# The second block's last eight gate projections: from the recurrent scan to one stretch ahead of the neighbourhood attention

## The chip, the cores and the metric

The kernel runs on one core of a Trainium2 chip. It is written for five engines and their queues: TensorE (PE, with its weight loads PEld), VectorE (DVE), ScalarE (ACT), GpSimd (POOL) and SyncE (SP), which issues most transfers. The metric is the device time of one execution in microseconds (us). Before the change it is 2379.51 us, the median of three runs (2378.23 to 2380.06).

## The reference

Two blocks work on 1024 tokens of 1024 features in float32. The first block has an attention layer with a window of 128 and sinks, and a layer of moving means over 2 to 16 tokens. The second puts 16 learned tokens in front, projects all 1040 once with a matrix of 6144 columns, and runs two mixers on the result, a neighbourhood attention (NA) and a gated linear recurrence in both directions. Two gates of 1024 columns each, the last 2048 of the projection, weigh the two mixers' outputs:

```python
def second_block(...):
    h = jnp.concatenate([meta_tokens, x], axis=1)            # 16 + 1024 tokens
    a = rms_norm(h, norm_mix[l])
    (q_na, k_na, v_na, q_hg, z_f, z_b, i_hg, g_hg, gate_na, gate_hg) = split_cols(a @ w_in[l])
    y_na = neighbourhood_attention(q_na, k_na, v_na, na_rpb[l]) @ w_na_out[l]
    y_hg = hgrn2_branch(q_hg, z_f, z_b, i_hg, g_hg, lb_all[:, l], hg_norm[l]) @ w_hg_out[l]
    mix = jax.nn.sigmoid(gate_na) * y_na + jax.nn.sigmoid(gate_hg) * y_hg
    h = h + mix @ w_o[l]
    m = rms_norm(h, norm_mlp[l])
    h = h + jnp.square(jax.nn.relu(m @ w_up[l])) @ w_down[l]

def chunk_scan(q, k, v, log_f):     # S_t = diag(f_t) S_(t-1) + k_t v_t^T,  o_t = S_t^T q_t
```

`gate_hg` is the gate of the second branch. It depends only on `a`, which is complete before the neighbourhood attention starts, and it is used only after the scan, where the branches are mixed.

## The kernel before, in words

**A float32 product in three parts.** Weights and activations are each split in a rounded high part and the rest, and `mm3` (L104) adds three matmuls for each product: high by high (L108), high weight by low activation (L110), low weight by high activation (L111). A weight block of 1024 rows by 128 columns goes through `w_cols`: one 512 KB load on SP (`wraw`, three buffers), a cast on ACT (`whi`, L79) and a subtraction on POOL (`wlo`, L80).

**A projection.** `pieces_fm` (L187) gives 128 columns of `a @ w_in` for all tokens, feature-major, as a list of pieces. With `cut=1` a piece is one half of the tokens: 8 row blocks by 3 matmuls of 512 columns, 24 in all, into one bank of the accumulator. With `cut=2` a piece is 12 matmuls, two pieces to a bank. The pieces of the forward forget projection work on the 1040 tokens in three parts, two of 264 and one of 512 (`MTOK`).

**A gate.** `gate` (L565) is such a projection of 128 of the 2048 gate columns: 48 matmuls, two ACT activations (L569) into a staging tile, two stores into `d_gate` in DRAM (L570). Gates 0 to 7 are `gate_na`, 8 to 15 `gate_hg`. Their results are read back much later, by the phases that mix the branches.

**Where the sixteen gates stand.** Gates 0 and 1 end the phase before NA: they use that phase's accumulator pool of four banks and its staging tiles `z`, and PE has nothing else between them. Gates 2 to 7 are fill in NA. Gates 8 to 15 are 32 pieces of 12 matmuls, fill in the scan, with the scan's accumulator pool `psm` of two banks and four staging tiles `gate`.

**The scan.** Four heads follow each other. `Head` holds what a head does: three `projections` (forget gates of both directions, with products F and K on DVE in `forget`, L1026; and the query, `QS`), `out_gate` (`gs`), `meta_state`, `begin`, seven `level`s on both halves of the tokens, four `states`, two `output`s and two `finish`es (in `ends`). One `level` on one half (L1121) is an ACT copy `kc` (two buffers), four 128-column float32 matmuls `A` (L1129), and on DVE a predicated copy (L1131), the products `K` (L1133) and `Q` (L1134) and a small `t` (L1137). The next level of that half needs this level's `Q` and `K`. `finish` transposes on PE (L1192) and multiplies on DVE (`oh`, L1195).

`weave` (L1211) issues the steps of one head and spreads a list of fill pieces over them evenly, by count. The fill of heads 0 to 2 is ten or nine gate pieces, the head's own `out_gate` and the three projections of the next head, which are what the next head starts from; the first `finish`es of the head before are put among the steps. Head 3's fill has the last four gate pieces, its `out_gate`, the reloading of NA's output and the products `y_na`.

**What sets the order.** The program is written in the order of these calls. A scheduler then orders each engine's queue by what is ready and what comes free, so a piece or a load can move some way from where it is written; buffers (three `wraw`, two banks `psm`, two `kc`) limit how far.

Of the kernel before, what the change touches and what calls it, by code (L numbers as in the profile page):

```python
# [30 lines left out]
def fused_kernel(tc, a, out, stop=None, dbg=None):  # L31
# [176 lines left out]
    def run(calls):  # L208
        for c_ in calls:
            c_()  # L210
# [72 lines left out]
    with lay:  # L283
        with ExitStack() as ph:
# [4 lines left out]
            psm = ph.enter_context(tc.tile_pool(name="psm", bufs=6 - SB, space=PSUM))  # L289
# [173 lines left out]
            fill, ss, tm_ = {}, {}, {}  # L463
# [37 lines left out]
        psm = xp.enter_context(tc.tile_pool(name="psm", bufs=4, space=PSUM))  # L501
# [63 lines left out]
    def gate(ps_pool, pool, g, cut=1, bufs=2, name="gate", w=None):  # L565

        def ev(ps, sl):
            st = pool.tile([P, T if name == "z" else 512], F32, name=name, bufs=bufs)[:, :512]
            nc.scalar.activation(out=st, in_=ps, func=AF.Tanh if g < 8 else AF.Sigmoid, scale=0.5 if g < 8 else 1.0)  # L569
            nc.sync.dma_start(out=d_gate[g][:, sl.start - NM:sl.stop - NM], in_=st)  # L570
        return pieces_fm(ps_pool, x2, lambda: w or w_cols(w2, 4096 + g * P), ev, TOK, cut)
# [3 lines left out]
    with ExitStack() as ph:  # L575
# [164 lines left out]
        feature_major(1)  # L740
        gate0[1]()
        gate1[1]()
        with tc.issue_after(last[3].ins):
            wk0_ = w_cols(w2, 512)
    xp.close()
# [230 lines left out]
    with ExitStack() as ph:  # L976
# [273 lines left out]

        head = Head(0)
        run(head.projections())
        gates = [p_ for g in range(8, 16) for p_ in gate(psm, gp, g, 2, GB)]
        last = []
        for hh in range(3):
            nxt = Head(hh + 1)
            n = (10, 9, 9)[hh]
            fill = gates[:4] + head.out_gate() + nxt.projections() + gates[4:n]
            gates = gates[n:]
            st = head.scan()  # L1260
            weave(st[:5] + last + st[5:], fill)
            last = head.ends()
            head = nxt
        oo = XT()
        og, ona_, ohg = head.out_gate(), [(i, d_na[i]) for i in range(4)], [(4 + i, d_hg[i]) for i in range(3)]
        fill = gates[:2] + og[:2] + [lambda: load_o(0, ona_)] + gates[2:] + og[2:] + [lambda: load_o(1, ona_)]
        fill += [lambda d_=d_ + i, hf=hf: y_na(d_, hf) for d_ in range(0, 8, 2) for hf in range(2) for i in range(2)]
        fill.insert(18, lambda: load_o(0, ohg))
        fill.insert(20, lambda: load_o(1, ohg))
        st = head.scan()  # L1270
        weave(st[:3] + last + st[3:-1], fill[:-4])
        for c_ in (fill[-4], st[-1], fill[-3], *head.ends(), fill[-2], fill[-1]):
# [596 lines left out]
```

## Time and profile before

| | |
|---|---|
| median of three runs | 2379.51 us |
| the profiled execution, its own time | 2379.98 us |
| its span | 2378.2 us |
| PE busy | 2309.6 us (97%), 12054 matmuls |
| DVE busy | 1426.5 us (60%) |
| ACT busy | 971.5 us (41%) |
| POOL busy | 791.5 us (33%) |
| scan: first head's transpose to the end of the fourth head | 1195.1 to 1590.0 us |
| two gates ahead of NA: their last matmuls | about 785 to 790 us |

The page gives busy time by engine over the whole span, the same in 40 slices, and the costliest groups of instructions. A group names its line, engine, operation, output and inputs, then busy time and mean duration of one, then the idle time ahead of it. Busy time counts an instruction from its start to its end, and successive instructions of an engine overlap, so that of PE's short matmuls the distance between two starts, and not the duration of one, tells how fast the engine gets on.

### The profile page before, as it was taken

The page shows a single profiled execution, that of the slowest core. Times are in us where ns is not written, and L with a number is a line of the kernel's source. Part 1 is how long each engine was busy: PE and PEld are TensorE (multiplying, and loading weights), DVE is VectorE, ACT ScalarE, POOL GpSimd, SP SyncE. Part 2 cuts the span into 40 slices and gives each one's busy share as a digit, 9 for nine tenths or more (in the row PEclk, how much of TensorE's full clock was granted, in tenths as well). Part 3 has the DMA queues.
Part 4 walks back from the last instruction along what each step waited for, and adds up shares of the span by engine and source line. Part 5 has one row for each costly group of instructions (what it writes and reads, how often), then busy time and mean ns, then how long its engine had stood idle before and what let it go on. Part 6 is the DMA issues. An engine that isn't in the chain of part 4 may idle for free. (4 is left out here: it accounts for less than half of the span.)

```text
span 2378.2 us, 32052 instructions
## 1 busy us (share of the span) xinstructions
PE 2309.6 (97%) x12054; PEld 1921.4 (81%) x12054; DVE 1426.5 (60%) x2602; ACT 971.5 (41%) x1808; POOL 791.5 (33%) x528
## 2 busy tenths in 40 slices
PE   7999999999999999999999999999989999999997
PEld 6877777888887888878988888877768888878886
DVE  5566677654367255553265746759784444786775
ACT  5344452422226454543232232423555555533334
POOL 2112123112226343431212112126354444444455
PEclk9999999999999999999999999999999999999999
DMA  5111103111124222211111111467235444754331
GB/s 160 36 28 36 28 27 108 40 45 58 40 63 138 62 68 67 54 58 45 46 52 54 41 54 54 139 200 258 71 120 199 146 151 164 267 220 168 107 124 71
DMA packets 237147, 230.01 MB, mean 97 GB/s; under 512 B 59896, under 2 KB 179022, under 8 KB 233408
## 3 DMA queue, kind: packets, MB, share of 16 engines
q1 hardware_dynamic: 228176, 210.31, 27.5%
q10 hardware_dynamic: 8224, 16.00, 1.8%
q0 software_dynamic: 592, 1.65, 0.3%
q8 instruction: 95, 1.56, 0.3%
q14 instruction: 60, 0.49, 0.1%
HBM read 168.68 MB, written 59.24 MB: 96 GB/s over the span
## 5 line engine op out<-in xcount | busy, mean ns | idle before, releaser
L108 PE MATMUL mm<-xh,whi 128*128 128x512 f32 (+2 forms) x1744 | 670.9, 385 | 8.5 <-DVE st L1544 3.7
L110 PE MATMUL mm<-xl,whi 128*128 128x512 f32 (+2 forms) x1744 | 665.3, 382 | 0.0
L111 PE MATMUL mm<-xh,wlo 128*128 128x512 f32 (+2 forms) x1744 | 662.3, 380 | 2.3 <-POOL wlo L80 2.2
L80 POOL TENSOR_TENSOR wlo<-wraw,whi 128x1024 fp32r<-128x1024 f32 (+1 forms) x127 | 300.2, 2369 | 894.3 <-ACT whi L79 838.4
L108 PEld LDWEIGHTS mm<-xh,whi 128*128 128x128 f32 x1744 | 329.2, 189 | 70.2 <-issue 3.5
L111 PEld LDWEIGHTS mm<-xh,wlo 128*128 128x128 f32 x1744 | 329.3, 189 | 66.1 <-POOL wlo L80 3.4
L110 PEld LDWEIGHTS mm<-xl,whi 128*128 128x128 f32 x1744 | 329.4, 189 | 56.2
L79 ACT CAST whi<-wraw 128x1024 fp32r<-128x1024 f32 (+1 forms) x127 | 128.9, 1018 | 371.8 <-PE mm L110 174.3
L111 PE MATMUL mm<-whi,xl 128*128 128x512 f32 (+1 forms) x688 | 247.8, 360 | 0.0
L110 PE MATMUL mm<-wlo,xh 128*128 128x512 f32 (+1 forms) x528 | 184.6, 350 | 3.3 <-POOL wlo L119 2.6
L108 PE MATMUL mm<-whi,xh 128*128 128x512 f32 (+1 forms) x528 | 184.7, 350 | 2.1 <-DVE X L281 1.3
L111 PEld LDWEIGHTS mm<-whi,xl 128*128 128x128 f32 x688 | 130.7, 190 | 19.3
L108 PE MATMUL mm<-whi,xl 128*128 128x512 f32 x352 | 138.5, 394 | 4.7 <-ACT whi L118 2.4
L110 PE MATMUL mm<-wlo,xl 128*128 128x512 f32 x352 | 138.8, 394 | 3.9 <-POOL wlo L119 3.9
L1668 POOL TENSOR_TENSOR wlo<-raw,whi 128x1024 fp32r<-128x1024 f32 (+1 forms) x42 | 84.1, 2003 | 100.8 <-ACT whi L1667 100.8
L110 PEld LDWEIGHTS mm<-wlo,xh 128*128 128x128 f32 x528 | 99.8, 189 | 17.2 <-POOL wlo L119 3.9
L108 PEld LDWEIGHTS mm<-whi,xh 128*128 128x128 f32 x528 | 99.8, 189 | 15.4 <-DVE X L281 1.7
L119 POOL TENSOR_TENSOR wlo<-wraw,whi 128x1024 fp32r<-128x1024 f32 x30 | 80.6, 2692 | 80.4 <-ACT whi L118 78.0
L1595 DVE TENSOR_TENSOR st<-st 128x512 f32<-128x512 f32 x64 | 61.1, 975 | 57.8 <-ACT st L1581 56.8
L1791 DVE TENSOR_TENSOR X<-X,mm 128x512 f32<-128x512 f32 x112 | 73.1, 680 | 37.2 <-PE mm L111 37.2
L878 DVE CUSTOM_DVE_ANT_0 s<-S,bi 128x400 f32<-128x400 f32 x64 | 34.5, 571 | 94.6 <-PE S L870 94.6
L119 DVE TENSOR_TENSOR pl<-PT,ph 100x512 fp32r<-100x512 f32 (+2 forms) x128 | 83.6, 668 | 10.3 <-ACT ph L118 9.3
(370 smaller groups left out, 4400.1 us busy)
## 6 DMA issues: line engine op xcount, KB each, us to landing
wraw<-in_w_in_dram SPq DMA_DIRECT2D x48, 512.0 KB, 3.8
d_S<-st SPq DMA_DIRECT2D x64, 256.0 KB, 4.7
raw<-in_w_up_dram SPq DMA_DIRECT2D x30, 512.0 KB, 5.0
d_A<-st ACTq DMA_DIRECT2D x48, 256.0 KB, 2.0
fa<-d_S SPq DMA_DIRECT2D x10, 1024.0 KB, 4.9
wraw<-in_pool_w_in_dram SPq DMA_DIRECT2D x18, 512.0 KB, 3.9
fa<-d_A SPq DMA_DIRECT2D x9, 1024.0 KB, 4.8
wraw<-in_attn_w_in_dram SPq DMA_DIRECT2D x32, 256.0 KB, 3.2
```

Source lines behind the costliest of these rows:

```text
L79: nc.scalar.copy(out=hv[:, i:i + n], in_=view[:, i:i + n])
L80: nc.gpsimd.tensor_tensor(out=lv[:, i:i + n], in0=view[:, i:i + n], in1=f(hv[:, i:i + n]), op=ALU.subtract)
L108: nc.tensor.matmul(ps, lhsT=lh[0], rhs=rh[0], start=first and i == 0, stop=False, skip_group_check=chain)
L110: nc.tensor.matmul(ps, lhsT=lh[0], rhs=rh[1], start=False, stop=False, skip_group_check=chain)
L111: nc.tensor.matmul(ps, lhsT=lh[1], rhs=rh[0], start=False, stop=last and i == n - 1, skip_group_check=chain)
L119: return (lo_eng or nc.vector).tensor_tensor(out=lo, in0=src, in1=f(hi), op=ALU.subtract)
L878: nc.vector.tensor_tensor_reduce(out=s, in0=sps[j], in1=bs[j], scale=-0.125, scalar=-NEG, op0=ALU.add, op1=ALU.min, accum_out=mx)
L1595: return nc.vector.tensor_tensor(out=out_, in0=x_, in1=y_, op=op)
L1668: nc.gpsimd.tensor_tensor(out=lv, in0=view, in1=f(hv), op=ALU.subtract)
L1791: added[:] = [nc.vector.tensor_tensor(out=dst, in0=dst, in1=banks[t], op=ALU.add)]
```

## The change

The eight gates 8 to 15 are computed right behind gates 0 and 1, each as two pieces of 24 matmuls, in that phase's accumulator pool and with its staging tiles `z`. The fill lists of the scan lose their 32 gate pieces; what remains is `out_gate` and the next head's projections in heads 0 to 2, and `out_gate`, the reloads and `y_na` in head 3. The two places at which NA's later outputs are reloaded in head 3's list move up by four, the number of pieces that went. The arithmetic of a gate is the same.

```diff
--- before.py
+++ after.py
@@ -740,6 +740,8 @@
         feature_major(1)
         gate0[1]()
         gate1[1]()
+        for g in range(8, 16):
+            run(gate(psm, up, g, name="z"))
         with tc.issue_after(last[3].ins):
             wk0_ = w_cols(w2, 512)
     xp.close()
@@ -1250,23 +1252,20 @@
 
         head = Head(0)
         run(head.projections())
-        gates = [p_ for g in range(8, 16) for p_ in gate(psm, gp, g, 2, GB)]
         last = []
         for hh in range(3):
             nxt = Head(hh + 1)
-            n = (10, 9, 9)[hh]
-            fill = gates[:4] + head.out_gate() + nxt.projections() + gates[4:n]
-            gates = gates[n:]
+            fill = head.out_gate() + nxt.projections()
             st = head.scan()
             weave(st[:5] + last + st[5:], fill)
             last = head.ends()
             head = nxt
         oo = XT()
         og, ona_, ohg = head.out_gate(), [(i, d_na[i]) for i in range(4)], [(4 + i, d_hg[i]) for i in range(3)]
-        fill = gates[:2] + og[:2] + [lambda: load_o(0, ona_)] + gates[2:] + og[2:] + [lambda: load_o(1, ona_)]
+        fill = og[:2] + [lambda: load_o(0, ona_)] + og[2:] + [lambda: load_o(1, ona_)]
         fill += [lambda d_=d_ + i, hf=hf: y_na(d_, hf) for d_ in range(0, 8, 2) for hf in range(2) for i in range(2)]
-        fill.insert(18, lambda: load_o(0, ohg))
-        fill.insert(20, lambda: load_o(1, ohg))
+        fill.insert(14, lambda: load_o(0, ohg))
+        fill.insert(16, lambda: load_o(1, ohg))
         st = head.scan()
         weave(st[:3] + last + st[3:-1], fill[:-4])
         for c_ in (fill[-4], st[-1], fill[-3], *head.ends(), fill[-2], fill[-1]):
```

Three places show the order of the engines before and with the change. A name with a number is one allocated tile; `z` and `gate` are staging tiles of gates, `wraw` weight loads, `mm` an accumulator bank, `xh` and `xl` the two parts of the activations. In the scan and after it, lines of the changed kernel between L742 and L1252 are two higher (its L1131 is the level's matmul, L1133, L1135 and L1136 its copy, K and Q, L1194 and L1197 the transposes and `oh` of `finish`, L1037 the product of `gs`).

The first is SP's queue at the end of the phase ahead of NA, before the change, from the store of gate 0's second half (`z_7143`) on:

```order
L570 DMA d_gate_4831<-z_7143 128x512
L60 DMA wraw_7590<-in_w_in_2_dram 128x8x128
L570 DMA d_gate_4831<-z_7171 128x512
L60 DMA wraw_7801<-in_w_in_2_dram 128x8x128
L794 DMA be_7246<-d_rpb_4832 16x16x48 x8
L794 DMA be_7255<-d_rpb_4832 16x16x48 x8
L570 DMA d_gate_4831<-gate_7587 128x512
L60 DMA wraw_8096<-in_w_in_2_dram 128x8x128
```

With the change, from the same store on:

```order
L570 DMA d_gate_4831<-z_7143 128x512
L60 DMA wraw_7422<-in_w_in_2_dram 128x8x128
L570 DMA d_gate_4831<-z_7171 128x512
L60 DMA wraw_7484<-in_w_in_2_dram 128x8x128
L570 DMA d_gate_4831<-z_7205 128x512
L570 DMA d_gate_4831<-z_7233 128x512
L60 DMA wraw_7546<-in_w_in_2_dram 128x8x128
L570 DMA d_gate_4831<-z_7267 128x512
L570 DMA d_gate_4831<-z_7295 128x512
L60 DMA wraw_7608<-in_w_in_2_dram 128x8x128
L570 DMA d_gate_4831<-z_7329 128x512
```

The bias rows `be` of NA stood behind gate 1's two stores and one more weight load; now the stores of eight gates stand there, each pair of stores with one weight load behind it or between. Gate 8 works with `wraw_7174`, which is issued ahead of these rows; `wraw_7422`, `wraw_7484`, `wraw_7546` and `wraw_7608` are those of gates 12 to 15, and the rows `z_7205` and `z_7233` are gate 8's stores.

The second is PE's queue in head 1, from the first level on. Before the change (where lines are left out, rows of the piece ahead of them follow):

```order
L1129 MATMUL A_12437<-Q_12377,kc_12435 128x128 x4
L108 MATMUL mm_12453<-xh0_6817,whi_12449 128x512
...
L1129 MATMUL A_12468<-Q_12408,kc_12466 128x128 x4
L108 MATMUL mm_12453<-xh0_6817,whi_12449 128x512
...
L1192 MATMUL tp_12493<-ident_67,kt_12260 128x128 x4
...
L1192 MATMUL tp_12514<-ident_67,kt_12313 128x128 x4
L108 MATMUL mm_12501<-xh1_7065,whi_12449 128x512
...
L1129 MATMUL A_12538<-Q_12377,kc_12536 128x128 x4
L108 MATMUL mm_12554<-xh0_6817,whi_12550 128x264
...
L1129 MATMUL A_12569<-Q_12408,kc_12567 128x128 x4
```

With the change, from the last matmul ahead of the first level on:

```order
L111 MATMUL mm_12745<-xh1_7065,wlo_12690 128x512
L1131 MATMUL A_12760<-Q_12706,kc_12758 128x128 x4
L1131 MATMUL A_12772<-Q_12733,kc_12770 128x128 x4
L108 MATMUL mm_12745<-xh1_7065,whi_12689 128x512
...
L111 MATMUL mm_12745<-xh1_7065,wlo_12690 128x512
L1194 MATMUL tp_12796<-ident_67,kt_12617 128x128 x4
L1194 MATMUL tp_12823<-ident_67,kt_12666 128x128 x4
L1131 MATMUL A_12857<-Q_12706,kc_12855 128x128 x4
L1131 MATMUL A_12869<-Q_12733,kc_12867 128x128 x4
L1131 MATMUL A_12894<-Q_12706,kc_12892 128x128 x3
L108 MATMUL mm_12810<-xh0_6817,whi_12806 128x264
```

Before, each half of a level (`A_12437` and `A_12468`, then `A_12538` and `A_12569`) is followed by a piece of its own: twelve matmuls of `out_gate` (`mm_12453`, `mm_12501`) or a projection piece (`mm_12554`); four of the nine gate pieces stand ahead of them and the rest behind the projections. With the change both halves of the first level follow each other, then twelve matmuls of `out_gate` (`mm_12745`) and the two transposes of the finished head (`tp`), then both halves of the second level (`A_12857`, `A_12869`) and three of four matmuls of the third level's first half (`A_12894`), with no piece between.

The third is DVE's queue at that place with the change:

```order
L1133 COPY_PREDICATED A_12707<-lvl_11298,A_12760 128x512
L1136 TENSOR_TENSOR Q_12706<-Q_12706,F_12225 128x256x2
L1133 COPY_PREDICATED A_12734<-lvl_11298,A_12772 128x512
L1136 TENSOR_TENSOR Q_12733<-Q_12733,F_12345 128x256x2
L1135 TENSOR_TENSOR K_12226<-K_12226,t0_12768 128x128x2x2
L1135 TENSOR_TENSOR K_12346<-K_12346,t0_12780 128x128x2x2
L1197 SCALAR_TENSOR_TENSOR oh_12801<-tp_12796,gn_11291,gs_12098 128x512
L1197 SCALAR_TENSOR_TENSOR oh_12828<-tp_12823,gn_11291,gs_12098 128x512
L1133 COPY_PREDICATED A_12707<-lvl_11298,A_12857 128x512
L1136 TENSOR_TENSOR Q_12706<-Q_12706,t0_12768 128x128x2x2
L1037 TENSOR_TENSOR gs_12730<-gs_12730,mm_12693 128x512
```

The rows A, Q and K of numbers 12707, 12706 and 12226 are of one half, those of 12734, 12733 and 12346 of the other. The product Q of the second level (`t0_12768`), for which the third level's matmuls on that half wait, stands behind both halves' copies and products of the first level, both `oh` of the finished head and the second level's copy; the two products of `gs`, which free the accumulator banks of `out_gate`, stand behind it.

## Rows read from the trace of the kernel before

**Rows 1.** The page: span, busy time, share and count of each engine, and PE's busy tenths and granted clock in 40 slices of the span.

```profile
span 2378.2 us, 32052 instructions
PE 2309.6 (97%) x12054; PEld 1921.4 (81%) x12054; DVE 1426.5 (60%) x2602; ACT 971.5 (41%) x1808; POOL 791.5 (33%) x528
PE   7999999999999999999999999999989999999997
PEclk9999999999999999999999999999999999999999
```

**Rows 2.** Windows: the projections ahead of head 0, then the four heads, each from its `meta_state` transpose to the next one's. Columns: window and length in us; busy us and instructions of PE, PEld, DVE, ACT, POOL; granted clock, DMA share, GB/s.

```profile
1165.00:1195.13 30.13, 30.13 (x143) 25.02 (x142) 17.76 (x36) 7.06 (x15) 9.57 (x5) 1.00 0.24 70
1195.13:1294.21 99.08, 99.08 (x562) 85.39 (x561) 61.20 (x117) 31.95 (x66) 19.91 (x9) 1.00 0.16 48
1294.21:1391.51 97.30, 97.30 (x559) 83.94 (x558) 60.05 (x124) 31.05 (x65) 17.54 (x8) 1.00 0.17 52
1391.51:1492.19 100.68, 99.00 (x562) 84.83 (x561) 60.49 (x124) 29.84 (x64) 17.85 (x8) 1.00 0.15 48
1492.19:1590.00 97.81, 95.10 (x526) 80.63 (x524) 70.68 (x126) 33.65 (x66) 14.69 (x6) 1.00 0.51 167
```

**Rows 3.** Windows of the same columns: the level section of each head, from its first level matmul to its last level's end.

```profile
1208.74:1264.00 55.26, 55.26 (x318) 48.58 (x317) 42.16 (x71) 17.99 (x32) 12.78 (x6) 1.00 0.15 43
1307.81:1364.06 56.25, 56.25 (x326) 49.37 (x324) 42.22 (x73) 17.18 (x31) 10.38 (x5) 1.00 0.14 43
1405.13:1461.97 56.84, 56.62 (x320) 48.81 (x319) 40.35 (x67) 16.67 (x31) 9.48 (x4) 1.00 0.12 38
1506.30:1552.97 46.67, 46.67 (x258) 40.55 (x257) 43.89 (x62) 20.16 (x33) 9.30 (x4) 1.00 0.58 190
```

**Rows 4.** Waits of PE in the windows of head 2 (the first two rows) and head 3 (the other two): engine, output and line of what waited, engine, tile and line of what it waited for, us in total, times, the longest.

```profile
PE mm L108 <- DVE QS L1035: 1.5, 1, 1.5
PE mm L108 <- ACT K L1028: 0.2, 1, 0.2
...
PE tp L1149 <- ACT kt L1146: 2.2, 1, 2.2
PE tp L1192 <- DVE kt L1183: 0.2, 1, 0.2
```

**Rows 5.** Timeline of PE in head 1: two matmuls of a projection piece ten steps apart, then matmuls of `level`. Columns: start in us, duration in us, engine, line, operation; at the end the number of records of one instruction group.

```profile
1301.57 0.39 PE L110 MATMUL mm<-xl,whi 128*128 128x512 f32 x1
...
1303.88 0.39 PE L111 MATMUL mm<-xh,wlo 128*128 128x512 f32 x1
...
1307.81 1.49 PE L1129 MATMUL A<-Q,kc 128*128 128x128 f32 x8
...
1311.90 1.49 PE L1129 MATMUL A<-Q,kc 128*128 128x128 f32 x8
...
1329.58 1.05 PE L1129 MATMUL A<-Q,kc 128*128 128x128 f32 x8
...
1331.93 1.05 PE L1129 MATMUL A<-Q,kc 128*128 128x128 f32 x8
...
1345.72 1.05 PE L1129 MATMUL A<-Q,kc 128*128 128x128 f32 x8
...
1349.38 1.05 PE L1129 MATMUL A<-Q,kc 128*128 128x128 f32 x8
```

**Rows 6.** Timeline of PE in the stretch of gates 0 and 1 ahead of NA: two matmuls 24 steps apart.

```profile
785.01 0.39 PE L110 MATMUL mm<-xl,whi 128*128 128x512 f32 x1
...
790.45 0.39 PE L110 MATMUL mm<-xl,whi 128*128 128x512 f32 x1
```

**Rows 7.** Groups of ACT in the scan: the gates' activations.

```profile
L569 ACT ACTIVATE gate<-mm 128x512 f32<-128x512 f32 x16 | 9.5, 595 | 20.1 <-PE mm L111 20.1
```

**Rows 8.** The page's groups of a weight block's subtraction and cast (count; busy us, mean ns of one; idle time ahead and what ended it), and its line of the weight loads (count, KB each, us from issue to landing).

```profile
L80 POOL TENSOR_TENSOR wlo<-wraw,whi 128x1024 fp32r<-128x1024 f32 (+1 forms) x127 | 300.2, 2369 | 894.3 <-ACT whi L79 838.4
L79 ACT CAST whi<-wraw 128x1024 fp32r<-128x1024 f32 (+1 forms) x127 | 128.9, 1018 | 371.8 <-PE mm L110 174.3
...
wraw<-in_w_in_dram SPq DMA_DIRECT2D x48, 512.0 KB, 3.8
```

**Rows 9.** Timeline of POOL: the first product with the bias rows `be` in NA, and one weight subtraction in head 1's levels.

```profile
817.06 1.15 POOL L801 TENSOR_TENSOR bm<-be,rm 128x576 f32<-128x576 f32 x1
...
1340.37 2.39 POOL L80 TENSOR_TENSOR wlo<-wraw,whi 128x1024 fp32r<-128x1024 f32 x1 [14.44 <-ACT whi L79]
```

**Rows 10.** Timeline of DVE in head 1's levels: copy, Q and K of one half, and the product F of `forget` twice, in brackets the idle time ahead.

```profile
1334.04 0.72 DVE L1131 COPY_PREDICATED A<-lvl,A 128x512 f32<-128x512 uint8 x1
1334.66 0.67 DVE L1134 TENSOR_TENSOR Q<-Q,t 128x512 f32<-128x512 f32 x1
1335.26 0.67 DVE L1133 TENSOR_TENSOR K<-K,t 128x512 f32<-128x512 f32 x1
...
1340.82 2.22 DVE L1030 TENSOR_SCALAR F<-F,lb 128x512 f32<-128x512 f32 x1 [2.24 <-ACT F L1027]
...
1346.56 0.55 DVE L1030 TENSOR_SCALAR F<-F,lb 128x512 f32<-128x512 f32 x1 [1.29 <-ACT F L1027]
```

**Rows 11.** Groups of DVE in head 1's level section, forms apart: the first levels' product Q and the finished head's `oh`.

```profile
L1134 DVE TENSOR_TENSOR Q<-Q,F 128x512 f32<-128x512 f32 x2 | 2.3, 1129 | 0.0
L1195 DVE SCALAR_TENSOR_TENSOR oh<-tp,gn,gs 128x512 f32<-128x512 f32 x2 | 1.5, 750 | 3.4 <-PE tp L1192 3.4
```

## The prediction

> **What bounds the kernel now.** The page comes first: TensorE (PE) is busy 97% of a span of 2378.2 us, hardly a slice falls under 9 tenths, and the granted clock is near full in every slice [rows 1]. So nothing is to be won from the clock, and little from PE's idle time as a whole. Next come the windows of the four scan heads, each from one `meta_state` transpose to the next [rows 2]. Heads 0 and 1 (99.08 and 97.30 us) show PE busy for all of their time; head 2 has 99.00 of 100.68, head 3 95.10 of 97.81. VectorE (DVE) has 60 to 61 us in each of the first three and 70.7 in the last. Within a head the work is uneven: the seven levels on both halves take 46.7 to 56.8 us, and in them DVE is busy 40 to 44 us [rows 3]. This second fact decides the forecast, because the change removes PE work there and no DVE work. Last come PE's own waits [rows 4]: 1.5 + 0.2 us in head 2, 2.2 + 0.2 in head 3, none in heads 0 and 1.
>
> A busy PE in these records need not be a PE that gets on, so head 2 is compared with head 1. Both issue the same matmuls (but for two that belong to head 3), and head 2 takes 100.68 − 97.30 = 3.4 us longer. The waits show 1.7 of these; the whole 3.4 is stall. With head 3's 2.4 the scan holds **5.8 us** of stall now.
>
> **The change part by part.**
>
> *The matmuls.* A gate is 48 matmuls of 512 columns, eight gates 384, and all move. In the scan ten start-to-start steps take 1303.88 − 1301.57 = 2.31 us, 0.231 each [rows 5]: 384 × 0.231 = 88.7 us leave it. The dense stretch's nearest rows are the gates already computed at that place: 24 steps between 785.01 and 790.45, 0.2267 each [rows 6], or 87.05 us added. The sum of both is **−1.65 us**. Bounds: if the stretch ran at the scan's rate, 0; nothing in the rows is faster than 0.2267.
>
> *No switching to save.* A level step is four fp32 matmuls in eight records. From one to the next with a piece of twelve matmuls between takes 1349.38 − 1345.72 = 3.66 us [rows 5], 0.89 more than 12 × 0.231. With pieces of 264 columns between them it is 2.35 us [rows 5], and these pieces, too, leave about 0.9. I take the switch as part of the step; steps remain, and so does it.
>
> *Evacuation, weights, stores.* ScalarE's (ACT) sixteen sigmoids on gates in the scan took 0.595 us each [rows 7]; a half gate in the stretch is 24 × 0.2267 = 5.4 us of matmuls, so they are covered. A gate's weights need a load (3.8 us to landing), a cast (1.0) and GpSimd's (POOL) subtraction (2.4) [rows 8], 7.2 us in a row, against 10.9 us of PE for a gate. The order of SP shows each load standing several gates ahead of its use, so PE's work on the gates between hides it. Without that cover it would cost up to 7.2 × 8 = 58 us. The stores go with their gates. Behind them on SP stand the bias rows `be` of the neighbourhood attention, moved back by the stretch's length like all that follows; POOL first uses them at 817.06 [rows 9], 26 us after the last gate step of [rows 6], so projections still hide their loads. Before the scan, four `gate<-d_gate` loads now stand on SP ahead of weights; the 30.13 us of head 0's projections [rows 2] cover them. I put these edits at 0; the upper bound is one load that comes out late, 3.8 us.
>
> *What the scan loses as cover.* Heads 0, 1 and 2 give up 120, 108 and 108 matmuls, head 3 the remaining 48. By PE's order 72 of them stood in the levels of heads 0 and 1: PE then needs 55.26 − 16.6 = 38.6 us and 56.25 − 16.6 = 39.6. In head 3's levels it is 36: 46.67 − 8.3 = 38.4. Against these stand 42.2, 42.2 and 43.9 us of busy DVE [rows 3]. Busy time counts DVE's overlap twice: a predicated copy, a Q and a K of one half take 0.72 + 0.67 + 0.67 = 2.06 us by duration, but start 0.62 and 0.60 apart [rows 10], so about 1.82. Some fifty large operations in a head's levels give back 0.08 to 0.1 each, and the real occupancy is near 37 us. On top of it, DVE is held up by POOL: the F product takes 2.22 us while a weight subtraction runs, and 0.55 without [rows 9, 10]. So DVE and PE come out almost level, 37 to 41 against 39, and stalls depend on places.
>
> I go through the new order with these durations and those of [rows 11], 0.1 off each for the overlap. In head 1, with the first level at 0: its two halves now stand back to back (1.32 each: 4.09 between starts less a piece of 2.77 [rows 5]), then twelve matmuls and two transposes, the second level at 6.15 and 7.1, the third's first half due at 8.05. DVE has copy, Q, copy, Q, K, K until 5.9, two `oh` until 7.25, copy until 7.9; then Q, for which the third level waits, would end at 8.5. But the weight buffer came free with the twelve matmuls at 5.4, so cast and subtraction run until 9.0, and Q ends at 9.6. PE stands about 1.6 us; behind the waiting level are the 264-column projections, whose bank is free only after the `gs` product at 10.2, another 0.3. A second subtraction later in the levels costs about 0.6. That gives 2.5 for heads 1 and 2 each, 1.5 for head 0 (no `oh`; one delayed Q, one later), and for head 3 its old 2.4 plus 0.7 where the first two levels stand together. Sum **9.6 us** against 5.8 now: **+3.8 us**. Bounds: 2.4 (all but head 3's kt wait goes), and 16.7, derived below.
>
> **The sum** is −1.65 + 3.8 = +2.2 us. The profiled execution took 2379.98 us (span 2378.2, 1.8 around it), 0.47 over the median of the three runs; I add to the median and round up for the many small places I have not followed: **2382.0 us**.
>
> **Rivals.**
>
> *DVE becomes the bound of the levels (slower).* If PE can't run ahead at all, each head's levels last as long as DVE's busy time: +42.2 − 38.6 = 3.6, 42.2 − 39.6 = 2.6 twice, 43.9 − 38.4 = 5.5, with the 2.4 us of head 3 16.7. Less 5.8 and 1.65 that is +9.25, or 2389 us. For it: DVE's rows in head 3 stand nearly end to end already [rows 3], and two queues this evenly loaded seldom both stay full. Against it: half levels 2.35 us apart went through without a wait of PE [rows 4, 5], and the new mean distance is 39.6 / 14 = 2.8. It decides if a half level costs DVE, with the projections' evacuations and POOL's delays, over 2.8 us. The Trainium skill (Perfetto Trace Analysis, section Optimization Strategy) says that regimes with different busiest engines may gain from being interleaved, which speaks against this change; by that rule the time would be this rival's. Chance 0.31.
>
> *The gates were in the way (faster).* Head 2's extra 3.4 us came where a late gate piece and a QS product held one of two banks [rows 4]. If heads without gates all run like head 1 without its gates, the change gives −1.65 − 3.4 = −5.1, 2374.5 us; with head 3's wait gone too, 2372. Against it: the same engines have less cover. Chance 0.08.
>
> *The stretch isn't dense.* If weights arrive late, it costs up to 58 us, 2438 us; the order speaks against it. Chance 0.03.
>
> *Forecast*: within 0.2% (4.8 us, about what a measurement of this kernel tells from no change). Chance 0.58.
>
> **Numbers.** Faster by over 0.2%: 0.08; within: 0.58; slower: 0.31 + 0.03 = 0.34. The range reaches from 2376.0 (between forecast and the faster case) to 2391.0 (the DVE case, with 2 us more), and leaves out some 0.1 on the faster side and 0.08 above. The forecast's own range is 2377 to 2384.
>
> **What would show it.** Right: a stretch of 87 us before the attention with steps of 0.227 and no PE wait on `wlo`; heads 0 to 2 of 73 to 75.5 us each, head 3 of 86 to 89; DVE over 80% busy in the levels, PE's waits there put down to DVE's Q or to `gs`. Wrong: heads of 77 us and more, with DVE full from the first to the last level (the DVE rival); heads 1 and 2 alike at 72.5 and no waits (the faster one); waits on POOL or on a load in the stretch (not dense); or a change outside the stretch and the scan, which no step here foresees.

## The result, and the profile after

The changed kernel takes **2389.92 us** (median of five executions, 2387.18 to 2392.43) against 2379.74 of the kernel before beside it: a ratio of 1.0043 (95% interval 1.0028 to 1.0058), 10.2 us slower. That is inside the range forecast (2376 to 2391), but not the likeliest case (2382, no change that can be told): it is the side of the slower rival, which was given 2389 us and a chance of 0.31. The experiments show that the rival's number came about by other causes than the rival's. That the range holds the time is luck in part: it reached that far for a case that did not come about.

The page of the profiled execution (2389.92 us too), span and busy times [rows 1]:

```profile
span 2388.2 us, 32074 instructions
PE 2312.6 (97%) x12054; PEld 1925.0 (81%) x12054; DVE 1410.8 (59%) x2602; ACT 973.3 (41%) x1809; POOL 796.7 (33%) x528
```

Nothing on this page tells where 10 us went; 97% is what it was. So the stages come next. First the stretch ahead of the attention, from the last transposes before the gates to the first score matmul of the attention. Timeline of PE, kernel before:

```profile
780.46 0.60 PE L175 MATMUL tp<-ident,pp 128*128 128x128 f32 x4
...
825.55 0.46 PE L870 MATMUL S<-kh,qh 64*128 64x400 f32 x2
```

and the changed kernel:

```profile
780.21 0.60 PE L175 MATMUL tp<-ident,pp 128*128 128x128 f32 x4
...
913.57 0.45 PE L872 MATMUL S<-kh,qh 64*128 64x400 f32 x2
```

45.09 us have become 133.36: the eight gates cost **88.27 us**, 0.2299 for each of 384 steps. Where each half of gate 8 and the first half of gate 9 begin:

```profile
790.65 0.40 PE L108 MATMUL mm<-xh,whi 128*128 128x512 f32 x1
...
796.23 0.40 PE L108 MATMUL mm<-xh,whi 128*128 128x512 f32 x1
...
801.68 0.40 PE L108 MATMUL mm<-xh,whi 128*128 128x512 f32 x1
```

The 24 steps of the first half take 5.58 us, 0.233 each, those of the second 5.45, 0.227 each, and so it goes on in all eight gates. Then the scan: windows of the four heads [rows 2] and of the level sections of heads 0, 1 and 3 [rows 3]. The last window ends at the same place of PE's queue as in [rows 2], now at 1599.01:

```profile
1283.14:1357.90 74.76, 72.31 (x443) 63.15 (x442) 56.28 (x110) 26.60 (x52) 14.22 (x7) 1.00 0.10 29
1357.90:1432.23 74.33, 72.82 (x451) 63.97 (x449) 58.29 (x122) 26.01 (x58) 12.61 (x7) 1.00 0.12 36
1432.23:1506.64 74.41, 72.90 (x452) 63.96 (x450) 58.25 (x126) 24.12 (x56) 8.78 (x5) 1.00 0.08 29
1506.64:1599.01 92.37, 86.84 (x483) 73.24 (x480) 70.35 (x133) 33.36 (x71) 17.04 (x6) 0.98 0.49 157
...
1293.99:1331.55 37.56, 36.55 (x234) 33.13 (x233) 32.79 (x57) 13.59 (x25) 6.43 (x3) 1.00 0.10 29
1368.74:1407.71 38.97, 37.46 (x242) 33.99 (x241) 33.92 (x62) 13.89 (x26) 5.59 (x3) 1.00 0.13 41
1521.11:1565.25 44.14, 39.14 (x213) 33.44 (x212) 39.78 (x56) 18.30 (x28) 13.87 (x5) 0.96 0.59 187
```

Heads 0 to 2 lost 24.32, 22.97 and 26.27 us, head 3 5.44: **79.0 us**, where 384 steps of 0.231 are 88.7. So 88.3 came and 79.0 went, +9.3 of the 9.9 us between the two profiled executions; the remaining 0.7 lies in the first block and behind the scan, which differ from execution to execution (below). By heads the stall grew by 120 × 0.231 − 24.32 = 3.4 us in head 0, 2.0 in head 1, −1.3 in head 2 (its old 3.4 went) and 11.1 − 5.4 = 5.7 in head 3. PE's waits in the scan [rows 4]:

```profile
PE A L1131 <- ACT kc L1128: 3.9, 4, 1.3
PE mm L111 <- POOL wlo L80: 3.6, 1, 3.6
PE A L1131 <- DVE Q L1136: 1.5, 4, 0.8
PE tp L1146 <- DVE Sf L1156: 1.4, 1, 1.4
```

These waits don't make up the whole stall: they are 2.4 us of head 0's 3.4 and 1.5 in heads 1 and 2 each, where 2.0 were lost; the rest is not put down to any wait. The longest single wait is in head 3. Timeline of that place (POOL, DVE, then PE; some rows between are left out):

```profile
1525.63 4.91 POOL L80 TENSOR_TENSOR wlo<-wraw,whi 128x1024 fp32r<-128x1024 f32 x1 [37.42 <-ACT whi L79]
...
1525.87 2.46 DVE L119 TENSOR_TENSOR xl<-wraw,xh 128x512 fp32r<-128x512 f32 x4
1528.25 0.72 DVE L1133 COPY_PREDICATED A<-lvl,A 128x512 f32<-128x512 uint8 x1
1528.87 2.22 DVE L1135 TENSOR_TENSOR K<-K,t 128x512 f32<-128x512 f32 x1
...
1530.59 0.73 PE L111 MATMUL mm<-xh,wlo 128*128 128x512 f32 x1 [3.59 <-POOL wlo L80]
1531.12 0.63 PE L108 MATMUL mm<-xh,whi 128*128 128x512 f32 x1
...
1534.11 0.40 PE L110 MATMUL mm<-xl,whi 128*128 128x512 f32 x1
```

The first weights of `y_na` are subtracted while DVE makes four low parts of the reloaded attention output. The subtraction takes 4.91 us instead of 2.4 [rows 8], longer by about the 2.46 of the low parts, and in its turn stretches K from 0.67 [rows 10] to 2.22: K ends at 1531.09, 0.55 us behind the subtraction. PE stands for 3.59 us. And it doesn't end there: the next matmuls start 0.43 apart, not 0.23. Windows of these microseconds, with the granted clock in the third column from the end:

```profile
1528.00:1530.00 2.00, 0.00 (x0) 0.00 (x0) 2.00 (x3) 0.00 (x0) 2.00 (x1) 1.00 0.85 256
...
1531.00:1532.00 1.00, 1.00 (x4) 0.71 (x4) 0.69 (x2) 0.83 (x2) 0.00 (x0) 0.50 0.38 109
...
1534.00:1535.00 1.00, 1.00 (x8) 0.81 (x7) 0.22 (x1) 0.31 (x1) 1.00 (x1) 0.95 0.36 137
```

After the wait PE is granted 0.50 of its clock (1.2 of 2.4 GHz), and the full clock again early in the window from 1534 on (0.95). The eight steps from 1530.59 to 1534.11 took 3.52 us for 8 × 0.231 = 1.85: 1.7 more. This one late weight block cost 5.3 us.

In heads 1 and 2 the place is the one that the prediction walked through, the third level's first half. Timeline of head 1 there:

```profile
1374.12 1.05 ACT L79 CAST whi<-wraw 128x1024 fp32r<-128x1024 f32 x1 [1.84 <-PE mm L110]
1376.18 0.62 ACT L1128 COPY kc<-K 128x512 f32<-128x512 f32 x1 [1.02 <-PE A L1131]
...
1377.67 0.62 ACT L1128 COPY kc<-K 128x512 f32<-128x512 f32 x1
...
1375.29 2.37 POOL L80 TENSOR_TENSOR wlo<-wraw,whi 128x1024 fp32r<-128x1024 f32 x1 [16.33 <-PE tp L1194]
...
1376.82 1.39 DVE L1136 TENSOR_TENSOR Q<-Q,t 128x512 f32<-128x512 f32 x1
...
1378.36 0.91 PE L1131 MATMUL A<-Q,kc 128*128 128x128 f32 x6 [1.25 <-ACT kc L1128]
```

Cast, then subtraction, then a Q of 1.39 us (0.67 without, [rows 10]) that ends at 1378.21. The profile puts PE's wait down to the `kc` that ends at 1378.29. But `kc` has two buffers, and this half's copy is the one of 1376.18, the first behind the two of the second level, over at 1376.80; the one of 1377.67 is the other half's. So it is Q, held up by the subtraction, that PE waits for, as the prediction has it.

### The profile page after: what moved, and what is told of

The parts are those of the page before. It is cut to its first block, busy times and chain, and to the rows that moved or that the text cites. A ratio compares the mean times of both kernels' runs of the same rounds, so it can differ in the third digit from the quotient of the medians.

```text
span 2388.2 us, 32074 instructions
## 1 busy us (share of the span) xinstructions
PE 2312.6 (97%) x12054; PEld 1925.0 (81%) x12054; DVE 1410.8 (59%) x2602; ACT 973.3 (41%) x1809; POOL 796.7 (33%) x528
## 3 DMA queue, kind: packets, MB, share of 16 engines
q0 software_dynamic: 592, 1.65, 0.3%
## 5 line engine op out<-in xcount | busy, mean ns | idle before, releaser
L119 POOL TENSOR_TENSOR wlo<-wraw,whi 128x1024 fp32r<-128x1024 f32 x30 | 83.3, 2779 | 79.8 <-ACT whi L118 74.3
L119 DVE TENSOR_TENSOR pl<-PT,ph 100x512 fp32r<-100x512 f32 (+2 forms) x128 | 83.6, 667 | 10.2 <-ACT ph L118 9.2
```

The lines of the kernel that those rows point to most:

```text
L119: return (lo_eng or nc.vector).tensor_tensor(out=lo, in0=src, in1=f(hi), op=ALU.subtract)
```

## The experiments

The theory, called "places" in the expectations: PE-bound work was moved, so no time is won or lost by moving it; the loss is stall at a few places, where the pieces left no longer stand between two dependent steps. The rival, "DVE bound": without gates the levels last as long as VectorE's work in them, whatever the order.

All times in us; "before" is the kernel before beside each. "Middle" is the difference of the traces from the last transpose ahead of the gates to the last output matmul of the scan.

| kernel | median | before | ratio, 95% interval | middle |
|---|---|---|---|---|
| changed kernel | 2389.92 | 2379.74 | 1.0043 (1.0028 to 1.0058) | +9.3 |
| e1 fill in levels | 2383.08 | 2379.32 | 1.0017 (1.0008 to 1.0026) | +1.9 |
| e2 weights first | 2383.44 | 2379.32 | 1.0022 (1.0013 to 1.0031) | +4.3 |
| e3 gate 15 back | 2383.78 | 2379.32 | 1.0023 (1.0012 to 1.0033) | +2.9 |
| e4 gate 15 only | 2386.00 | 2379.32 | 1.0029 (1.0020 to 1.0038) | +7.7 |
| e5 both fixes | 2378.53 | 2378.77 | 0.9996 (0.9987 to 1.0005) | −1.8 |
| e6 both, head 3 by weight | 2377.36 | 2378.77 | 0.9996 (0.9987 to 1.0005) | −0.5 |
| e7 before, 10 8 10 | 2376.48 | 2378.77 | 0.9993 (0.9984 to 1.0002) | −3.4 |
| e8 gates twice | 2471.70 | 2378.77 | 1.0386 (1.0372 to 1.0401) | +88.5 |
| e9 split on VectorE | 2381.01 | 2378.76 | 1.0005 (0.9996 to 1.0015) | +2.1 |
| e10 e5 and e9 | 2378.47 | 2378.76 | 0.9997 (0.9987 to 1.0006) | −5.1 |
| e11 e10 again | 2377.00 | 2378.66 | 0.9992 (0.9983 to 1.0001) | −4.0 |
| e12 e7, split on VectorE | 2379.19 | 2378.66 | 1.0005 (0.9995 to 1.0014) | −2.5 |

The middle is the sharper measure: heads 0 to 2 of e10 and e11, one kernel traced twice, agree within 0.03 us, and those of the kernel before and of e8 are 99.08, 97.30 and 100.7 in both. Head 3 does not repeat so well: in e10 and e11 it took 75.72 and 76.66, so that a difference of 1 us in the middle tells nothing. The last transpose ahead of the gates stands anywhere from 777.9 to 783.1 in these traces, and what follows the scan's last transposes lasts 789.4 to 794.8.

**Spread the fill (e1).** In `weave`, for heads 0 to 2:

```diff
...
-                while done * len(steps) < (i + 1) * len(fill):
+                while done * sum(cost) < sum(cost[:i + 1]) * len(fill):
...
-            weave(st[:5] + last + st[5:], fill)
+            weave(st[:5] + last + st[5:], fill,
+                  [0, 1, 1] + [2] * 2 + [0] * len(last) + [2] * 12 + [1] * 4 + [1] * 2)
```

> The changed kernel with the fill of heads 0 to 2 spread by weight instead of by count: two shares for each half level, one for each begin, state and output, none for meta_state and finish. Same work, same eight gates ahead of the attention. Theory 'places': the scan loses its time at the few places where matmuls of two level halves stand together (waits for kc and Q of 0.92 + 0.42 in head 0, 1.43 + 0.42 in head 1, 1.42 + 0.42 in head 2, 5.0 us in all); with a piece behind each half they go, and heads 0 to 2 are 1.3, 1.8 and 1.8 us shorter: 2385 us. Some of it may come back at the states and outputs, which lose fill: up to 1.5 us each head. Rival 'DVE bound': the levels last as long as VectorE's work in them, whatever stands between; heads stay at 74.3 to 74.8 us, waits move to other levels: 2390 us.

Measured 2383.08. The heads of this kernel, and head 1's level section:

```profile
1360.35:1405.56 45.21, 45.21 (x279) 40.60 (x278) 38.38 (x71) 16.24 (x30) 6.17 (x3) 1.00 0.11 36
...
1283.38:1355.07 71.69, 71.44 (x443) 62.97 (x441) 53.81 (x98) 25.92 (x52) 13.75 (x7) 1.00 0.10 30
1355.07:1427.64 72.57, 72.34 (x451) 63.95 (x449) 57.77 (x124) 25.61 (x58) 12.53 (x7) 1.00 0.12 37
1427.64:1499.77 72.13, 72.13 (x451) 63.94 (x449) 57.39 (x129) 23.87 (x56) 8.95 (x5) 1.00 0.09 30
```

3.1, 1.8 and 2.3 us less; the waits in the levels are gone, and head 0's for `Sf` (1.4) is down to 0.25. VectorE is 85% busy in head 1's levels and holds nobody up. Nothing but the order of the pieces was changed, so without that order these stalls don't arise; e9 shows what else it takes.

**Head 3's weights (e2).** The first weights of `y_na` ahead of the reloads:

```diff
-        fill = og[:2] + [lambda: load_o(0, ona_)] + og[2:] + [lambda: load_o(1, ona_)]
+        def first_weights():
+            wn[0], wn[1] = pair_cols(w_na, 0)
+        fill = og[:2] + [first_weights, lambda: load_o(0, ona_)] + og[2:] + [lambda: load_o(1, ona_)]
```

(and the later two insertions one place on).

> The changed kernel with the first weights of y_na loaded and split ahead of the first reload of the attention's output, instead of behind both reloads; nothing else. Theory 'late weights in head 3': PE's wait of 3.6 us for wlo goes, since the subtraction (4.9 us beside four low parts on VectorE) no longer stands behind the reloads; head 3 is 3.0 to 3.9 us shorter: 2386.3 us. Rival 'head 3 is bound by VectorE': the wait moves to another tile (xl of the reloads, Q or kc) and less than 1 us is won: 2389 us or more.

Measured 2383.44. PE's waits in head 3, and its window to the last output matmul (82.2 us in the changed kernel):

```profile
PE A L1131 <- DVE Q L1136: 1.2, 1, 1.2
PE A L1131 <- ACT kc L1128: 0.7, 1, 0.7
```

```profile
1509.18:1586.50 77.32, 75.34 (x438) 64.64 (x436) 63.86 (x114) 29.05 (x59) 12.31 (x5) 1.00 0.55 167
```

4.9 us less, more than the 3.0 to 3.9 expected: with the wait the half clock went too (1.00 in the window). One new wait for Q of 1.2 us came.

**Which gate costs what (e3, e4).** e3 leaves gate 15 in head 3; against the changed kernel:

```diff
-        for g in range(8, 16):
+        for g in range(8, 15):
...
-        fill = og[:2] + [lambda: load_o(0, ona_)] + og[2:] + [lambda: load_o(1, ona_)]
+        gates = gate(psm, gp, 15, 2, GB)
+        fill = gates[:2] + og[:2] + [lambda: load_o(0, ona_)] + gates[2:] + og[2:] + [lambda: load_o(1, ona_)]
```

(and the later two insertions where they were before). e4 does the reverse; against the kernel before:

```diff
+        run(gate(psm, up, 15, name="z"))
...
-        gates = [p_ for g in range(8, 16) for p_ in gate(psm, gp, g, 2, GB)]
+        gates = [p_ for g in range(8, 15) for p_ in gate(psm, gp, g, 2, GB)]
...
-        fill = gates[:2] + og[:2] + [lambda: load_o(0, ona_)] + gates[2:] + og[2:] + [lambda: load_o(1, ona_)]
+        fill = og[:2] + [lambda: load_o(0, ona_)] + og[2:] + [lambda: load_o(1, ona_)]
```

(and the later two insertions as in the change).

> Gates 8 to 14 ahead of the attention as in the change, gate 15 back among the fill of head 3 as before. Theory 'places': head 3 has its old order and its old stall (2.3 us) in place of 5.9, the other heads stay: 2386.3 us, and no wait of PE for wlo in head 3. Rival 'every gate costs alike': the 10.2 us of the whole change are spread over eight gates, 1.3 us for this one: 2388.6 us.

> The complement: gate 15 alone ahead of the attention, gates 8 to 14 in heads 0 to 2 of the scan as before. Theory 'places': head 3 alone loses its cover, with the 3.6 us wait for wlo: 2379.7 + 3.6 = 2383.3 us. Rival 'every gate costs alike': 2381.0 us. The gains of this kernel and of the one with gate 15 back should add up to the whole change, 10.2 us.

2383.78 and 2386.00: gate 15 alone costs 6.7 us, the seven others 4.5; together 11.1, the whole 10.2. It is far from alike. Head 3 with gate 15 back, to the last output matmul; no wait for `wlo` is left in it, and its wait for `kt` is 1.4 (2.2 in the kernel before):

```profile
1493.74:1581.05 87.31, 85.90 (x487) 73.70 (x484) 65.77 (x114) 31.07 (x62) 14.63 (x6) 1.00 0.53 167
```

and without gate 15, the others in the scan:

```profile
1500.85:1585.65 84.80, 78.75 (x438) 67.21 (x437) 61.87 (x107) 29.33 (x53) 16.87 (x6) 0.96 0.55 174
```

To the same matmul head 3 of the kernel before takes 87.6; 84.80 is 2.8 us less for 11.1 us of matmuls taken out. Its waits are 3.0 for `wlo` and 2.8 put down to `kc`, its clock 0.96. I had expected 3.6 for e4 from the wait alone; the `kc` wait and the half clock were not in it.

**Both (e5), and head 3 too (e6).** e5 joins the two edits; e6 adds

```diff
-        weave(st[:3] + last + st[3:-1], fill[:-4])
+        weave(st[:3] + last + st[3:-1], fill[:-4],
+              [1, 1, 1] + [0] * 2 + [1] * 14 + [1] * 4 + [1])
```

> The changed kernel with both edits of the first experiments: fill of heads 0 to 2 by weight (one piece behind each half level), and the first weights of y_na ahead of the reloads in head 3. Theory 'places': the two losses are apart in time and add up. Heads as in the two traces, 71.7 + 72.6 + 72.1 + 77.3 = 293.7 us where the changed kernel has 305.7: 12 us less, 2378 us, level with or just under the kernel before. Rival 'DVE bound': what one fix wins the other loses, since VectorE's queue is the limit in sum: 2383 us as with each alone.

> As the kernel with both fixes, and head 3's fill by weight as well: one share for meta_state, each begin, half level, state and output, none for the two finishes. What is left of head 3's waits (Q 1.36, kc 0.82) stands where two halves follow each other; one such place goes. Theory 'places': 1 us under the kernel with both fixes, 2377 us. Rival: head 3 is at its bound by VectorE, no difference.

2378.53: the fixes add up, as expected. Heads 71.71, 72.56, 72.59 and 77.80 us. e6's 2377.36 cannot be told from it, and its trace does not show the 1 us that I expected: head 3 is 79.07, 1.3 longer, with a wait for Q of 1.5 and one for `kt` of 1.9.

**The kernel before had a stall of its own (e7).**

```diff
-            n = (10, 9, 9)[hh]
+            n = (10, 8, 10)[hh]
```

> The kernel before with 10, 8 and 10 gate pieces in heads 0, 1 and 2 in place of 10, 9 and 9: no gate is cut between two heads, its accumulator bank isn't held across the border. Eight gates stay in the scan. Theory: head 2's extra 3.4 us against head 1 came from a half gate that held one of two banks; head 2 then takes 97.3 us like head 1: 2379.5 - 3.4 = 2376 us. Rival: the stall is due to VectorE and moves: 2379 us.

2376.48. Heads 1 and 2:

```profile
1291.94:1386.41 94.47, 94.47 (x546) 81.65 (x545) 60.16 (x124) 30.45 (x64) 17.38 (x8) 1.00 0.16 51
1386.41:1486.38 99.97, 99.97 (x570) 86.16 (x569) 59.10 (x124) 30.93 (x65) 16.98 (x8) 1.00 0.15 51
```

A piece is 12 × 0.231 = 2.77 us; with one fewer head 1 is 2.83 shorter, and head 2 with one more is 0.71 shorter instead of 2.77 longer: 3.5 us of stall are gone, and PE waits for nothing in it. Two pieces fill a bank. With 10 and 9 pieces the border between heads 1 and 2 falls in the middle of a bank, with 10 and 8 it does not (a gate, four pieces, is still cut behind head 0, but between two banks). That the half-filled bank was held is argued from the code; what e7 shows is that the stall goes with the odd piece. The changed kernel won these 3.4 us as well; it wasn't the gates that were in the way but how they were dealt out.

**The added half alone (e8).** The kernel before, the gates computed twice (`to` is where the stores go):

```diff
         gate1[1]()
+        for g in range(8, 16):
+            run(gate(psm, up, g, name="z", to=d_spare))
```

> The kernel before, unchanged in the scan, and the eight gates computed a second time ahead of the attention into a DRAM tensor that nothing reads: the added half of the change alone. The step sized it 87.05 us (384 steps of 0.2267); the trace of the changed kernel has its attention 88.0 us later. Expected 2379.5 + 88 = 2467.5 us, with heads as before (99.1, 97.3, 100.7, 87.6). If the scan's relief in the changed kernel were short for another reason than the order of the scan, such as the loads of the attention or of the scan coming late behind the stretch, the attention or the scan would be longer here too.

2471.70. The stretch is 88.27 us by its trace, the attention as long as ever (272.8 us from its first to its last score matmul), and the four heads 99.08, 97.30, 100.71 and 87.79: nothing of the loss comes from the stretch or from loads behind it. The rest of the +92.9 lies in the ends, which vary; four executions make it no sharper.

**Subtractions on VectorE (e9, e10, e11, e12).** On the changed kernel (e9), on e5 (e10, e11) and on e7 (e12), from head 0's projections (the expectation says head 1's) to the end of the scan:

```diff
+    where = [nc.gpsimd]
...
-            nc.gpsimd.tensor_tensor(out=lv[:, i:i + n], in0=view[:, i:i + n], in1=f(hv[:, i:i + n]), op=ALU.subtract)
+            where[0].tensor_tensor(out=lv[:, i:i + n], in0=view[:, i:i + n], in1=f(hv[:, i:i + n]), op=ALU.subtract)
...
         head = Head(0)
+        where[0] = nc.vector
         run(head.projections())
...
+        where[0] = nc.gpsimd
```

> The changed kernel with the weight subtractions of the scan on VectorE instead of GpSimd, from head 1's projections on. VectorE gets four blocks of 1024 columns more in a head, some 1.25 us each by its low parts of 512 columns (0.62), 5 us; GpSimd gives up 2.4 us each. Theory 'places': heads 0 to 2 change by no more than 1 us in sum and the wait at the third level stays or shrinks, because VectorE has idle time in a head and its products are no longer stretched while GpSimd subtracts (Q 1.39 there, 0.67 elsewhere); in head 3 the 4.9 us subtraction goes and the wait for wlo falls from 3.8 to about 3: heads 74.8, 74.3, 74.4 and 81 us, 2388 us. Rival 'DVE bound': 5 us more of VectorE in each head show as 3 to 5 us more in each head, 2400 us or over.

> The same on the kernel with both fixes, whose heads 0 to 2 stand at 71.7, 72.6 and 72.6 us, within 0.5 us of no stall. Theory 'places': with a piece behind each half level there is room for 5 us more on VectorE; each head within 1 us of these: 2379 us. Rival: with the pieces spread VectorE has become the limit, and its added work shows in full: 74 us and more in each head, 2385 us or over.

2381.01 and 2378.47. I had expected no more than 1 us in heads 0 to 2 of e9; it was 5.6. Its heads 0 and 1:

```profile
1285.32:1356.86 71.54, 71.54 (x443) 63.01 (x442) 55.62 (x114) 26.43 (x52) 3.20 (x2) 1.00 0.11 30
1356.86:1429.93 73.07, 72.54 (x452) 63.90 (x449) 58.13 (x128) 26.02 (x58) 2.93 (x2) 1.00 0.12 37
```

DVE groups of about head 1 (1355 to 1432 us in both traces), changed kernel:

```profile
L1136 DVE TENSOR_TENSOR Q<-Q,t 128x512 f32<-128x512 f32 x12 | 9.3, 777 | 0.0
...
L1032 DVE TENSOR_SCALAR F<-F,lb 128x512 f32<-128x512 f32 x3 | 4.9, 1624 | 1.8 <-ACT F L1029 1.8
```

and e9:

```profile
L1138 DVE TENSOR_TENSOR Q<-Q,t 128x512 f32<-128x512 f32 x12 | 8.7, 722 | 0.0
L82 DVE TENSOR_TENSOR wlo<-wraw,whi 128x1024 fp32r<-128x1024 f32 x5 | 6.1, 1221 | 2.2 <-PE A L1133 1.4 <-ACT whi L81 0.8
...
L1034 DVE TENSOR_SCALAR F<-F,lb 128x512 f32<-128x512 f32 x3 | 1.6, 543 | 0.5 <-ACT F L1031 0.5
```

VectorE took over five blocks of 1.22 us in this stretch, and head 1 got 1.3 us shorter. F fell from a mean of 1.62 to 0.54 us and Q from 0.78 to 0.72, and VectorE's busy time in head 1 is what it was (58.29 and 58.13): what the blocks cost it, it no longer loses beside GpSimd. So e9 does not add to VectorE's load as I had meant it to, and the test of the rival is e1. What e9 does show is what the subtractions on GpSimd cost: without them heads 0 to 2 are 5.6 us shorter with the fill in the order of the change. At the third level of head 1 a wait of 0.53 for Q is left of 1.25. With the fill of e5 they cost less, 0.4 us in each of heads 0 to 2 and 1.1 to 2.1 in head 3 (e10, e11): heads 0, 1 and 3 of e10, the latter to its last output matmul,

```profile
1284.06:1355.35 71.29, 71.29 (x442) 62.97 (x441) 53.61 (x103) 25.90 (x52) 2.64 (x2) 1.00 0.10 30
1355.35:1427.54 72.19, 72.19 (x452) 63.96 (x450) 57.31 (x130) 25.63 (x58) 2.64 (x2) 1.00 0.13 37
...
1499.68:1575.40 75.72, 74.91 (x438) 64.79 (x436) 62.32 (x123) 29.19 (x59) 4.72 (x2) 1.00 0.55 171
```

with 72.1 in head 2: PE shows busy for all of these first three heads. Last, whether that kernel's stages repeat, and whether GpSimd's subtractions cost the scan before too:

> The kernel with both fixes and the scan's subtractions on VectorE once more, for its time: by the trace its stages from the last transpose ahead of the gates to the end of the scan are 794.0 us against 799.0 of the kernel before, 5 us less, while its median was only 0.3 us less. Theory 'stages repeat, the ends vary': the four heads come out at 71.3, 72.2, 72.1 and 75.7 us again, within 0.2, and the median falls toward 2374 to 2376 us. Rival: the heads differ from execution to execution, and the first trace was a lucky one.

> The kernel before with 10, 8 and 10 gate pieces and the scan's subtractions on VectorE: gates stay in the scan. Theory 'cover': with the gates between, what GpSimd's subtractions cost VectorE was hidden behind TensorE's matmuls already, so taking them away wins nothing in heads 0 to 2 (99.1, 94.5, 100.0 us as with 10, 8, 10 alone, within 0.3); 2376.5 us. Rival: the collisions cost the scan before as well, by 1 to 3 us a head as in the changed kernel: 2372 us or less.

e11: 71.31, 72.18 and 72.17 us again, head 3 76.66 where it had been 75.7; median 2377.00. e12: heads 0 to 2 of

```profile
1193.28:1292.32 99.04, 99.04 (x563) 85.39 (x562) 60.85 (x124) 31.96 (x66) 2.62 (x2) 1.00 0.16 48
1292.32:1386.74 94.42, 94.42 (x546) 81.64 (x545) 62.06 (x130) 30.44 (x64) 3.79 (x2) 1.00 0.16 51
```

and 99.91 against 99.06, 94.47 and 99.97 of e7: with the gates between, taking the same collisions away wins nothing in heads 0 to 2 (head 3 is 88.8 for 87.8, no more than it may differ by itself). They were there before, and covered.

*Open.* By the middle of the traces e10 and e11 should be 4 to 5 us faster than the kernel before; their medians are 0.3 and 1.7. Their profiled executions (2375.12 and 2375.65, against 2379.98) do differ by that much; where the other executions, which have no trace, lose it was not found. No version here is shown to beat the kernel before: of e7, e10 and e11 each interval still holds 1.

## Why the prediction was right and wrong

**The bound** was read right: PE's clock and idle time gave nothing, the scan's waits decided. "Nothing is to be won from the clock" was true and misleading: it can be lost, by a stall that the change makes.

**The matmuls**: −1.65 forecast, −0.4 measured (88.27 − 88.7). The 24 steps of 0.2267 [rows 6] were the second half of gate 1, and were taken for a whole gate: in the stretch first halves go at 0.233 and second halves at 0.227, 0.2299 in the mean. The cast and the subtraction of a weight block, which stand over the first halves here, are not enough to explain it: in the kernel before, a cast from 785.43 and a subtraction from 786.56 to 788.96 stand over the very steps of [rows 6]. Why first halves are slower is open.

**Weights, stores, evacuation at 0**: right. No wait of PE in the stretch, the attention unchanged at 272.8 us.

**The cover lost by the scan**: +3.8 forecast, +9.7 measured; this is the step that failed, in two of four heads. Heads 1 and 2 were right in place and cause, and nearly in size: of the 1.6 at the third level 1.25 came, of the 0.6 for a later subtraction 0.26 (a Q behind an F of 2.11), of the 0.3 for the bank of `gs` nothing; 2.0 of stall in each for 2.5. Head 0 was put at 1.5, of which waits of 0.76 and 0.26 for Q came, and lost 3.4: the wait for `Sf` at the states (1.4, behind an F of 2.22 beside a subtraction) was not followed, since I walked through the levels alone. Head 3 was put at +0.7 and lost 5.7; its 92.4 us lie outside the 86 to 89 that were to show the forecast right. I carried its old wait over and looked only at the two levels that stand together, though the list of fill in the diff shows what had stood in front of `y_na`: the gate pieces were the time in which its first weights came. I named what covers the gates' own weights, and not what had covered the weights of the work behind them. Nor had the sum a term for the clock: the wait of 3.6 us cost 5.3 with the slower matmuls behind it. This wait, its half clock and the two of 0.7 put down to `kc`, less the old 2.2 for `kt`, are 4.5 of the 5.7; the rest is not put down to any wait.

**The DVE rival** had the time (2389) and not the mechanism. By it heads were to take 77 us and more, with DVE full; heads 0 to 2 took 74.3 to 74.8, with DVE 87% busy in the levels. And e1, which takes no work from DVE, removes the stalls with DVE at 85%. (The levels lost more matmuls than the 72 of the prediction, 84 in heads 0 and 1 each by the windows, so PE had even less to do there.) The Trainium skill (Perfetto Trace Analysis, section Optimization Strategy) says that regimes with different busiest engines may gain from being interleaved. By the time of the change alone that would hold (10.2 us lost by taking them apart), but most of that was the place of single pieces: with each side mended in its own way, the middle is −1.8 apart (e5) and −3.4 interleaved (e7), with the subtractions on VectorE −5.1 and −4.0 apart (e10, e11) and −2.5 interleaved (e12), and no median tells these kernels from the kernel before. Whether interleaving as such gains here is not shown.

**The faster rival** ("the gates were in the way") was half true: head 2's 3.4 us went, as it said, and e7 gets them without the change.

**What the collisions are.** GpSimd's subtraction and VectorE's operations on SBUF hold each other up: F 2.1 to 2.2 and 0.55 us, K 2.22 and 0.67, the subtraction itself 4.91 and 2.4. The Trainium skill (SBUF — State Buffer, section Who interferes with whom) says that the two share one pair of ports under an exclusive lock, and that a VectorE instruction with two inputs in SBUF contends with a GpSimd instruction that reads SBUF; the traces agree, the lengthening of 2.5 us by four low parts of 2.46 above all. The prediction had the effect [rows 9, 10], and its walk through the third level put 1.1 of the 1.6 us down to it (Q at 9.6 in place of 8.5), which e9 bears out (0.53 left of 1.25). It did not look for it at the states of head 0 and in head 3. e1 and e9 together say what a stall of heads 0 to 2 takes: a collision, and a place where no piece covers it; to take away either was enough for most of it.

## What to carry to other kernels

When work is moved out of a stage that TensorE bounds, its own time only changes address; price instead every dependent step that it stood in front of, the next weight block's load, cast and subtraction first, and walk through each kind of section, not the densest alone. Spread what fill is left by the steps that need cover rather than evenly by count: that gave back most of the loss here. And where fill is dealt out in pieces of a bank, let no bank be cut at a border.

## What was not expected of the hardware

- A wait of 3.59 us of PE in head 3, in a stretch that was busy on both sides, was followed by a granted clock of 0.50 until 1534, at 0.43 us a step; the waits of 2.56 us in e9 and 2.99 in e4 in the same part of head 3 were followed by half clock too, and so was one of 2.10 late in head 3 of e4. Waits of 2.2 us in head 3 of the kernel before and of 2.3 in that of e8 were not.
- Once started, GpSimd's subtraction can be the one that is held up: 4.91 us, when four VectorE operations stand back to back.
- PE's 512-column steps are 0.233 us in the first half of each added gate and 0.227 in the second, eight times over; the cause is open.
